# Weights of the projections split by two DMAs from DRAM, in place of a load, a copy and a subtraction

## The chip, the cores and the metric

The kernel runs on one core of one Trainium2 chip. The metric is the device time of one execution in microseconds: a median of 1206.1 us over three runs (1205.3 to 1206.65) before the change. Times, spans and rows come from one profiled execution, unless a text says that they are of the runs.

## The reference: what is computed

One encoder block over 1024 tokens of width 1024, in float32. The tokens form a grid of 16 rows by 64 columns.

```
n    = rmsnorm(h) ; proj = n @ w_in                    # 1024 x (3072 + 32) columns
y_na = neighbourhood attention of proj's qa, ka, va    # 8 heads x 64
y_gl = bidirectional gated linear attention            # 4 heads, chunks of 64 tokens
h    = h + concat(y_na, y_gl) @ w_out
h    = h + square(relu(rmsnorm(h) @ w_ff1)) @ w_ff2    # 4096 wide
out  = rmsnorm(h)
```

## The kernel before

**Products in parts.** TensorE works on operands of the type F32R, which holds fewer bits than float32. Each operand is therefore kept as a high part (the value rounded to F32R) and a low part (what the rounding left over, again as F32R), and each product is three matmuls: high by high, high weight by low data, low weight by high data (`product`). In names, `wh` and `wl` are the parts of a weight block, `nh` and `nl` those of the normed input, `y` those of the mixer's output.

**Blocks of weights.** The columns of `w_in` and of `w_out` lie in DRAM as blocks of 128 columns, each 128 partitions by 1024 float32 (512 KB): 24 blocks of `w_in` and 8 of `w_out`. A block of `w_in` serves two halves of 512 tokens with 24 matmuls each (`proj`; tile name `proj`). The output projection (`sums`; tile name `op`) goes through the 8 blocks of `w_out` twice, once for each half of the tokens: in the first pass with 21 matmuls a block, since the last of the eight slices of its input is left out until it is ready, in the second with 24. The missing slice is added between the passes from a rearranged tile of its own (tile name `opl`, weights loaded at L905 and split by `split`).

**How a block is made.** `weights` loads it into a float tile `wf` (a DMA from SP, L165) and calls `split`: ScalarE copies it to `wh` (L173), which rounds, and GpSimd, or VectorE in three cases, writes `wl = wf - wh` (L174). `wf`, `wh` and `wl` have two buffers each, in the pool `stg`. So `wf` of a block can be loaded while two earlier blocks are still in use, and its parts can be written when TensorE is through with the block before the last one. Two blocks of `w_in` at the start, and the rearranged slice, go through `load_w` or L905 and `split` without `weights`.

**Order of the work.** TensorE's instructions stand in the order in which the program is written. On the other engines a scheduler sets the order by priorities; what is written under `tc.high_priority(offset=SOON_W)` goes in as if it had been written some 100 instructions earlier. Each engine then works through its own instructions in order, and so do the DMA queues: SP's, which carries nearly all loads, and GpSimd's, whose DMAs stand in one line with its arithmetic.

**Stages.** Up to 44 us the input is split and normed and the first two blocks are projected. Then the linear attention runs head by head, with projections of later blocks put between its steps (`Fill`) so that TensorE has work while VectorE and ScalarE are at gates, scans and norms (to about 262 us). The neighbourhood attention follows in the same manner, in four pairs of heads (to about 441 us), and beside its last pair the first pass of the output projection begins. From about 465 us on the output projection stands nearly alone, until 545 us; the MLP takes the rest, from weight tiles (`A`) of its own that SP loads. GpSimd sums the squares for the second norm in the middle of the output projection (L880), as soon as VectorE has added a slice to `hT` and ScalarE has squared it.

Of the kernel before, what the change touches and what calls it, by code (L numbers as in the profile page):

```python
# [10 lines left out]
F32 = mybir.dt.float32  # L11
F32R = mybir.dt.float32r
U32 = mybir.dt.uint32
AF = mybir.ActivationFunctionType
ALU = mybir.AluOpType
# [3 lines left out]
P = 128  # L19
D = 1024  # L20
# [43 lines left out]
def block_kernel(ctx, tc, xT, g_mix, w_in, w_z, rpb, na_mask, gu, gb, g_gla, sel_f, sel_b,  # L64
                 rst, w_out, g_ff, w1, w2, g_fin, out):
    nc = tc.nc
    V, S, DMA, G = nc.vector, nc.scalar, nc.sync, nc.gpsimd
# [11 lines left out]
    stg = stg_stack.enter_context(pool("stg", L, 2))  # L79
# [81 lines left out]
    def weights(block, eng=None):  # L161

        with tc.high_priority(offset=SOON_W):
            wf = stg.tile([P, D], F32, tag="wf", name="wf")
            DMA.dma_start(wf, block)  # L165
            return split(wf, eng)

    def split(wf, eng=None, steps=1):
        wh = stg.tile([P, D], F32R, tag="wh", name="wh")
        wl = stg.tile([P, D], F32R, tag="wl", name="wl")  # L170
        for i in range(steps):
            c = slice(i * D // steps, (i + 1) * D // steps)
            S.copy(wh[:, c], wf[:, c])  # L173
            (eng or V).tensor_tensor(wl[:, c], wf[:, c], wh[:, c].bitcast(F32), op=ALU.subtract)  # L174
        return wh, wl
# [51 lines left out]
    def proj(blk, evac):  # L227

        w = weights(w_in[blk], G)
        for hf in range(2):  # L230
            d = bank("mm", f"proj{blk}_{hf}")
            yield from proj_part(d, w, hf * H, H)
            evac(hf, d)
# [437 lines left out]
    def sums(hf, d, ks, eng=None, w=None, ahead=()):  # L671

        w = w or weights(w_out[d], eng)
        o = bank("mm", f"op{hf}_{d}")
        for i, _ in enumerate(out_mm(o, hf, w, ks)):
            to_parts(hf, ahead[i:i + 1], G)
            yield
        add(hf, d, o)
# [220 lines left out]
    yhl[1] = half(a3, "y1")  # L899
    fill.run()  # L900
    w10 = weights(w_out[0], G)

    wf = stg.tile([P, D], F32, tag="wf", name="wf")
# [581 lines left out]
```

## Time and profile before

| what | profiled execution |
|---|---|
| time of this execution | 1203.34 us (the runs' median is 1206.1) |
| span of the core | 1201.6 us |
| TensorE busy | 1156.0 us, 96% |
| VectorE, ScalarE, GpSimd busy | 896.8, 646.3, 282.6 us |
| GpSimd's subtractions at L174 | 36, 88.8 us, 2467 ns each on the mean |
| loads of `wf` by SP | 38 of 512 KB through `weights`; 4 of 256 KB and 1 of 512 KB by others |
| moved by all DMAs | 73.02 MB, mean 61 GB/s |
| of that, by GpSimd's queue | 0.93 MB |
| granted TensorE clock, mean | 0.991 |

The rows are read so: a group's row names line, engine and operation, what is written and read, the count, then busy time, the mean of one in ns, and the idle time of that engine just before. A row of the order of time has start and duration in us, and in square brackets the idle time ahead of it and what ended it. A matmul's duration of some 0.39 us is longer than the distance between two starts, since matmuls are pipelined. In a row of a stretch stand its bounds, its length, then each engine's busy time with its count of instructions (TensorE's matmuls, its weight loads, VectorE, ScalarE, GpSimd), the granted TensorE clock, the DMA engines' share and GB/s.

### The profile page before, as it was taken

The page shows a single profiled execution, that of the slowest core. Times are in us where ns is not written, and L with a number is a line of the kernel's source. Part 1 is how long each engine was busy: PE and PEld are TensorE (multiplying, and loading weights), DVE is VectorE, ACT ScalarE, POOL GpSimd, SP SyncE. Part 2 cuts the span into 40 slices and gives each one's busy share as a digit, 9 for nine tenths or more (in the row PEclk, how much of TensorE's full clock was granted, in tenths as well). Part 3 has the DMA queues.
Part 4 walks back from the last instruction along what each step waited for, and adds up shares of the span by engine and source line. Part 5 has one row for each costly group of instructions (what it writes and reads, how often), then busy time and mean ns, then how long its engine had stood idle before and what let it go on. Part 6 is the DMA issues. An engine that isn't in the chain of part 4 may idle for free.

```text
span 1201.6 us, 15423 instructions
## 1 busy us (share of the span) xinstructions
PE 1156.0 (96%) x5632; PEld 946.8 (79%) x5632; DVE 896.8 (75%) x1558; ACT 646.3 (54%) x1201; POOL 282.6 (24%) x199
## 2 busy tenths in 40 slices
PE   9998999899999999999999999999999999999995
PEld 8877777687877878877778888888888888888775
DVE  8787778767868785695858885877859768597467
ACT  6766565545555665444643635546355463454654
POOL 5311101122131323530103230412304114041003
PEclk9999999999999999999999999999999999999998
DMA  7111010110111142230210122111211122111203
GB/s 236 50 58 52 25 36 19 35 57 19 49 36 49 32 156 92 104 123 1 70 59 26 58 70 69 35 55 53 71 53 35 53 70 70 53 36 53 71 1 140
DMA packets 37259, 73.02 MB, mean 61 GB/s; under 512 B 8928, under 2 KB 20320, under 8 KB 37184
## 3 DMA queue, kind: packets, MB, share of 16 engines
q1 hardware_dynamic: 36608, 71.11, 17.7%
q8 instruction: 44, 0.72, 0.2%
q0 software_dynamic: 432, 0.93, 0.2%
q14 instruction: 31, 0.25, 0.1%
q10 hardware_dynamic: 144, 0.00, 0.0%
HBM read 67.84 MB, written 5.96 MB: 61 GB/s over the span
## 4 chain that ended last, share of the span: by engine, by line
PE 70%; DVE 18%; ACT 8%; issue 2%; DMA 1%; SPq 0%; POOL 0%; DVEq 0%; ACTq 0%
PE f L111 24%; PE u L111 21%; PE proj L111 12%; PE op L111 5%; PE sc L111 2%; PE no L111 2%; PE pt L116 1%; DVE st L569 1%; DVE nl L284 1%; DVE b L492 1%; DVE b L490 1%; DVE st L566 1%; DVE pl L958 1%; DVE nf L888 1%; DVE fsq L1388 1%
## 5 line engine op out<-in xcount | busy, mean ns | idle before, releaser
L958 POOL TENSOR_TENSOR ul<-uB,uh 128x512 fp32r<-128x512 f32 x84 | 109.2, 1319 | 330.4 <-ACT uh L993 213.4
L980 ACT CAST ph<-A 128x512 fp32r<-128x512 f32 x166 | 103.0, 621 | 146.2 <-PE f L111 73.6
L174 POOL TENSOR_TENSOR wl<-wf,wh 128x1024 fp32r<-128x1024 f32 x36 | 88.8, 2467 | 333.8 <-ACT wh L173 310.6
L111 PE MATMUL f<-uh,ph 128*128 128x512 f32 x400 | 155.8, 390 | 1.5 <-ACT u L1001 1.4
L111 PE MATMUL f<-ul,ph 128*128 128x512 f32 x400 | 155.7, 389 | 0.1
L111 PE MATMUL f<-uh,pl 128*128 128x512 f32 x400 | 155.7, 389 | 0.0
L958 DVE TENSOR_TENSOR pl<-A,ph 128x512 fp32r<-128x512 f32 x166 | 112.8, 689 | 52.6 <-ACT ph L980 52.6
L111 PE MATMUL proj<-nh,wh 128*128 128x512 f32 x352 | 150.9, 429 | 0.8 <-DVE qd L255 0.8
L111 PE MATMUL proj<-nh,wl 128*128 128x512 f32 x352 | 139.6, 397 | 0.0
L111 PE MATMUL proj<-nl,wh 128*128 128x512 f32 x352 | 139.4, 396 | 0.0
L1140 DVE TENSOR_TENSOR hT<-hT,f 128x512 f32<-128x512 f32 x168 | 113.0, 687 | 19.9 <-PE f L111 19.9
L111 PE MATMUL u<-n,ph 128*128 128x512 f32 x288 | 89.2, 391 | 2.0 <-ACT ph L893 2.0
L111 PEld LDWEIGHTS f<-uh,ph 128*128 128x128 f32 x400 | 75.1, 188 | 17.9 <-ACT u L1001 1.8
L111 PEld LDWEIGHTS f<-ul,ph 128*128 128x128 f32 x400 | 75.1, 188 | 16.0 <-DVE ul L958 0.4
L111 PEld LDWEIGHTS f<-uh,pl 128*128 128x128 f32 x400 | 75.1, 188 | 15.6
L111 PEld LDWEIGHTS proj<-nh,wh 128*128 128x128 f32 x352 | 66.9, 190 | 19.8 <-issue 5.2
L993 ACT CAST uh<-uB 128x512 fp32r<-128x512 f32 x84 | 51.9, 618 | 51.3 <-PE f L111 34.5
L111 PE MATMUL u<-T,ph 128*128 128x512 f32 x256 | 79.2, 391 | 0.1
L111 PEld LDWEIGHTS proj<-nh,wl 128*128 128x128 f32 x352 | 67.1, 191 | 15.2
L111 PEld LDWEIGHTS proj<-nl,wh 128*128 128x128 f32 x352 | 67.4, 191 | 11.5 <-issue 1.4
L111 PE MATMUL op<-y,wh 128*128 128x512 f32 x240 | 75.8, 396 | 0.4 <-DVE y L665 0.4
L111 PE MATMUL u<-nt,ph 128*128 128x512 f32 x224 | 68.9, 389 | 0.0
(297 smaller groups left out, 2484.5 us busy)
## 6 DMA issues: line engine op xcount, KB each, us to landing
A<-in_w SPq DMA_DIRECT2D x64, 512.0 KB
wf<-in_w_in SPq DMA_DIRECT2D x22, 512.0 KB
wf<-in_w_out SPq DMA_DIRECT2D x17, 512.0 KB
hT<-in_xT SPq DMA_DIRECT2D x2, 2048.0 KB
xs<-in_xT SPq DMA_DIRECT2D x6, 512.0 KB
out<-hT SPq DMA_DIRECT2D x4, 512.0 KB
out<-hT SPq DMA_DIRECT2D x8, 256.0 KB
rpb<-rpb SPq DMA_DIRECT2D x16, 96.0 KB
```

What stands on the lines that cost most here:

```text
L111: m = nc.tensor.matmul(*args, **kw)
L116: tc.keep_in_program_order(nc.tensor.transpose(*args, **kw))
L174: (eng or V).tensor_tensor(wl[:, c], wf[:, c], wh[:, c].bitcast(F32), op=ALU.subtract)
L284: V.scalar_tensor_tensor(nl[:, k, sl], xs[:, k, :], gmix[:, k:k + 1], nh[:, k, sl].bitcast(F32), op0=ALU.mult, op1=ALU.subtract)
L490: V.tensor_tensor_scan(b[0:64, c], rsts[0:64, :], m[0:64, :], 0.0, op0=ALU.mult, op1=ALU.add)
L492: V.tensor_tensor_scan(b[64:128, c][:, ::-1], rsts[64:128, ::-1], m[64:128, ::-1], 0.0, op0=ALU.mult, op1=ALU.add)
L566: V.scalar_tensor_tensor(st[0:64, i + 1, :], st[0:64, i, :], dec[0:64, i:i + 1], st[0:64, i + 1, :], op0=ALU.mult, op1=ALU.add)
L569: V.scalar_tensor_tensor(st[64:128, j - 1, :], st[64:128, j, :], dec[64:128, j:j + 1], st[64:128, j - 1, :], op0=ALU.mult, op1=ALU.add)
L958: return kp(eng.tensor_tensor(l, x, h.bitcast(F32), op=ALU.subtract))
L980: kp(S.copy(ph, x))
L993: kp(S.copy(uh, x))
L1140: kp(V.tensor_tensor(hT[:, d, c], hT[:, d, c], o[:, s], op=ALU.add))
```

## The change

`weights` no longer loads a float tile and no longer calls `split`. A DMA from GpSimd's queue brings the block from DRAM into `wh` and casts it to F32R on the way. ScalarE writes `-wh` into `wl`. A second DMA from GpSimd's queue reads the same block from DRAM once more and adds it to what stands in `wl`, so that `wl` becomes block minus high part. The argument that named the engine of the subtraction is not used any more. `split` stays as it is for the two blocks at the start and for the rearranged slice. All 38 calls of `weights` are changed: 22 for `w_in`, 16 for `w_out`.

```
     def weights(block, eng=None):
 
         with tc.high_priority(offset=SOON_W):
-            wf = stg.tile([P, D], F32, tag="wf", name="wf")
-            DMA.dma_start(wf, block)
-            return split(wf, eng)
+            wh = stg.tile([P, D], F32R, tag="wh", name="wh")
+            wl = stg.tile([P, D], F32R, tag="wl", name="wl")
+            G.dma_start(wh, block)
+            S.activation(wl, wh.bitcast(F32), AF.Copy, scale=-1.0)
+            G.dma_start(wl, block, accum_op=ALU.add)
+            return wh, wl
```

The line numbers behind `weights` move up by 3 (L174 becomes L177, L880 becomes L883).

GpSimd in the output projection, before: the last low parts ahead of the sums of squares, and the first of the seven sums (`acc` is the sum, `sq` a square).

```order
L174 TENSOR_TENSOR wl<-wf,wh 128x1024 [waits DMAHW3_49,PE_49,Activation_49]
L174 TENSOR_TENSOR wl<-wf,wh 128x1024 [waits DMAHW4_49,PE_49,Activation_49]
L174 TENSOR_TENSOR wl<-wf,wh 128x1024 [waits DMAHW5_49,PE_49,Activation_49]
L880 TENSOR_TENSOR acc_4603<-acc_4603,sq_4610 128x512 [waits Activation_49]
L880 TENSOR_TENSOR acc_4603<-acc_4603,sq_4618 128x512 [waits Activation_49,Pool_49]
L880 TENSOR_TENSOR acc_4603<-acc_4603,sq_4626 128x512 [waits Activation_49,Pool_49]
```

The same place now, from the slice's subtraction (L177) to the end of the sums.

```order
L177 TENSOR_TENSOR wl<-wf,wh 128x1024 [waits DMASW4_49,DMAHW0_49,PE_49,Activation_49]
L166 DMA wh<-in_w_out 128x1024 [waits DMASW5_49,PE_49]
L883 TENSOR_TENSOR acc_4572<-acc_4572,sq_4579 128x512 [waits Activation_49]
L883 TENSOR_TENSOR acc_4572<-acc_4572,sq_4587 128x512 [waits Activation_49,Pool_49]
L168 DMA wl<-in_w_out 128x1024 [waits DMASW6_49,Activation_49]
L166 DMA wh<-in_w_out 128x1024 [waits DMASW3_49,PE_49]
L883 TENSOR_TENSOR acc_4572<-acc_4572,sq_4595 128x512 [waits Activation_49,Pool_49]
L883 TENSOR_TENSOR acc_4572<-acc_4572,sq_4603 128x512 [waits Activation_49,Pool_49]
L883 TENSOR_TENSOR acc_4572<-acc_4572,sq_4611 128x512 [waits Activation_49,Pool_49]
L883 TENSOR_TENSOR acc_4572<-acc_4572,sq_4619 128x512 [waits Activation_49,Pool_49]
L883 TENSOR_TENSOR acc_4572<-acc_4572,sq_4627 128x512 [waits Activation_49,Pool_49]
L168 DMA wl<-in_w_out 128x1024 [waits Activation_49]
```

Where one subtraction stood for a block, two DMAs stand, high part and low part in turn, and the sums of squares now lie between the two DMAs of a block: two of the seven in the first pair, five in the second.

ScalarE at the end of the last attention pair, before: the copies to `wh` between the attention's casts (`pt`) and copies (`otmp`).

```order
L173 CAST wh<-wf 128x1024 [waits DMAHW0_49,PE_49,Pool_49]
L782 CAST pt_3936<-pt_7_0_4375 128x2x128 [waits PE_49,Activation_49]
L782 CAST pt_3938<-pt_7_1_4380 128x2x128 [waits PE_49,Activation_49]
L173 CAST wh<-wf 128x1024 [waits DMAHW1_49,PE_49,Pool_49]
L173 CAST wh<-wf 128x1024 [waits DMAHW2_49,PE_49,Pool_49]
L812 COPY otmp<-no_0_1_4344 64x512 [waits PE_49]
L812 COPY otmp<-no_1_1_4347 64x512 [waits PE_49]
```

And now: the negations, which wait for GpSimd's DMAs (`DMASW`).

```order
L167 ACTIVATE wl<-wh 128x1024 [waits DMASW5_49,DMASW2_49,PE_49]
L785 CAST pt_3914<-pt_7_0_4349 128x2x128 [waits PE_49,Activation_49]
L785 CAST pt_3916<-pt_7_1_4354 128x2x128 [waits PE_49,Activation_49]
L167 ACTIVATE wl<-wh 128x1024 [waits DMASW7_49,DMASW4_49,PE_49]
L815 COPY otmp<-no_0_1_4319 64x512 [waits PE_49,Activation_49]
L167 ACTIVATE wl<-wh 128x1024 [waits DMASW6_49,DMASW1_49]
L815 COPY otmp<-no_1_1_4322 64x512 [waits PE_49,Activation_49]
```

Here one negation stands an instruction later than its copy did. The matmuls are the same, in the same order.

## The prediction

> **What bounds the kernel now.** I read the page's busy times and its chain first, then the busy times by stretch of the program, then the waits of the weights' tiles.
>
> ```profile
> PE 1156.0 (96%) x5632; PEld 946.8 (79%) x5632; DVE 896.8 (75%) x1558; ACT 646.3 (54%) x1201; POOL 282.6 (24%) x199
> PE 70%; DVE 18%; ACT 8%; issue 2%; DMA 1%; SPq 0%; POOL 0%; DVEq 0%; ACTq 0%
> core 0: us, PE busy (x) PEld busy (x) DVE busy (x) ACT busy (x) POOL busy (x), PEclk, DMA share, GB/s
> 44.00:262.00 218.00, 200.73 (x1113) 160.64 (x1112) 167.76 (x262) 127.79 (x206) 39.62 (x28) 0.97 0.12 39
> 262.00:441.00 179.00, 176.34 (x909) 141.03 (x909) 141.06 (x386) 106.62 (x266) 42.45 (x24) 1.00 0.14 44
> 441.00:465.00 24.00, 23.60 (x125) 18.69 (x125) 18.99 (x55) 14.46 (x40) 7.79 (x4) 1.00 0.60 218
> 465.00:545.00 80.00, 77.03 (x340) 62.38 (x338) 52.66 (x63) 35.49 (x53) 36.92 (x19) 1.00 0.28 99
> ```
>
> TensorE sets the end: busy 96%, and 70% of the chain. The four stretches are the linear attention with its projections (44 to 262 us), the neighbourhood attention with its own (to 441), and the output projection, first beside the last attention work (to 465) and then alone (to 545). TensorE idles 17 us in the first (218 less 200.7) and 3 us in each of the second and the last. So little can be gained, and whatever makes TensorE wait for a weight shows in full.
>
> When is a weight late? Its two parts live in two buffers each, so the block after next can be made only when a block's last matmul is through. The time left is one block's length on TensorE.
>
> ```profile
> 263.60 1.05 ACT L173 CAST wh<-wf 128x1024 fp32r<-128x1024 f32 x1 [1.95 <-PE proj L111]
> 276.67 1.05 ACT L173 CAST wh<-wf 128x1024 fp32r<-128x1024 f32 x1 [0.69 <-PE proj L111]
> 312.33 1.05 ACT L173 CAST wh<-wf 128x1024 fp32r<-128x1024 f32 x1
> 328.60 1.05 ACT L173 CAST wh<-wf 128x1024 fp32r<-128x1024 f32 x1 [1.97 <-PE proj L111]
> 448.14 1.05 ACT L173 CAST wh<-wf 128x1024 fp32r<-128x1024 f32 x1 [1.17 <-PE op L111]
> 455.76 1.05 ACT L173 CAST wh<-wf 128x1024 fp32r<-128x1024 f32 x1 [1.92 <-issue]
> 491.15 1.05 ACT L173 CAST wh<-wf 128x1024 fp32r<-128x1024 f32 x1 [3.71 <-PE op L111]
> 496.60 1.05 ACT L173 CAST wh<-wf 128x1024 fp32r<-128x1024 f32 x1 [4.39 <-PE op L111]
> 492.29 2.39 POOL L174 TENSOR_TENSOR wl<-wf,wh 128x1024 fp32r<-128x1024 f32 x1 [2.37 <-ACT wh L173]
> 477.97 0.39 PE L111 MATMUL op<-y,wl 128*128 128x512 f32 x1
> 478.20 0.40 PE L111 MATMUL op<-y,wh 128*128 128x512 f32 x1
> PE op L111 <- POOL wl L174: 2.8, 2, 1.8
> ```
>
> ScalarE's copies that waited for TensorE mark the releases. In the projections of the attention they are 13 to 16 us apart (263.60 to 276.67, 312.33 to 328.60), because attention work runs between a block's matmuls; where the output projection begins, 7.6 (448.14 to 455.76); and later there 5.45 us (491.15 to 496.60), which is 24 matmuls of 0.23 us (478.20 less 477.97). Today's chain fits even there: the float weight lies ready, the copy takes 1.05 and GpSimd's subtraction, 0.09 behind it, 2.39, in all 3.5 us. TensorE waits 2.8 us for it in the last stretch.
>
> **The change part by part.** It removes 38 loads on SP, 35 subtractions on GpSimd and 3 on VectorE. ScalarE's 38 copies become 38 negations of the same size. GpSimd's queue gets 76 DMAs of 512 KB, strictly high part, low part, high part; nothing can be fetched ahead of the release any more. The new chain from release to use is a DMA, a negation and a second DMA.
>
> The trace has no casting and no adding DMA. The nearest rows are the plain ones on GpSimd's queue:
>
> ```profile
> guf<-in_gu POOLq DMA_DIRECT2D x1, 256.0 KB, 6.3
> rsts<-in_rst POOLq DMA_DIRECT2D x1, 256.0 KB, 8.5
> msk<-in_na_mask POOLq DMA_DIRECT2D x1, 256.0 KB, 3.4
> selF<-in_sel_f POOLq DMA_DIRECT2D x1, 64.0 KB, 3.4
> selB<-in_sel_b POOLq DMA_DIRECT2D x1, 64.0 KB, 3.1
> 0.00:25.00 25.00, 22.53 (x133) 20.76 (x133) 20.07 (x35) 18.35 (x39) 15.50 (x17) 1.00 0.88 281
> ```
>
> The mask's 256 KB took 3.4 us in a quiet stretch; guf and rsts took 6.3 and 8.5 in the first 25 us, where the DMA engines were 88% busy at 281 GB/s. At that rate 256 KB more are 0.93 us.
> - Casting DMA: 3.4 + 0.93 = 4.3 us. Low end 3.1 (selB), high end 9.4 (rsts and 0.93). I take 4.3, since the mask was moved beside the same work.
> - Negation: 1.05 us, some 0.1 of handover on each side, 0.25 for ScalarE's queue: 1.5.
> - Adding DMA: it must read the old value too. Second stream free: 4.3; both streams in turn: 3.4 - 0.93 + 4 x 0.93 = 6.2; high end 9.4 again. I take 5.8, nearer the doubled stream.
>
> Together 11.6 us; TensorE can run two matmuls with the high part first, so 11.1 count.
>
> *The Trainium skill, "DMA: Bandwidth & Descriptors", section "Anatomy of one DMA — SWDGE (gpsimd) path", fits such a DMA as 2.0 us plus the bytes at 436 GB/s. By that fit each DMA would be an estimated 3.2 us, which is a rival below; for the mask it gives 2.6, and the row above says 3.4.*
>
> Attention projections, 44 to 441 us: 13 to 16 us are there and 11.1 are needed, so 0; the cover is the attention work between a block's matmuls. Without it the length would be 48 matmuls of 0.23, 11.0 us, and the chain would just show. Behind an adding DMA that waits, GpSimd's queue holds the clearing of state tiles and the low parts of the next queries; GpSimd is busy 40 of 218 us and 42 of 179 there, so I cost that at nothing.
>
> The first block behind the opening has no cover:
>
> ```profile
> L111 PE MATMUL sb<-nh,wl x32: 279/283/415, 11.4 to 36.8; 128*128 128x256 f32 x32
> L111 PE MATMUL proj<-nh,wl x352: 387/393/632, 44.2 to 436.5; 128*128 128x512 f32 x176
> ```
>
> Its buffer comes free at 37.1, and its low part was first used at 44.2. New: 37.1 + 11.6 = 48.7, so 4.5 us late. **+4.5.**
>
> The output projection alone, 465 to 545:
>
> ```profile
> 465.00:545.00 80.00, 66.64 (x214) 39.93 (x214) 5.55 (x3) 13.39 (x13) 24.04 (x10) 1.00 0.28 99
> ```
>
> This is the same stretch for the instructions on the high part alone: 214 matmuls, which are 5 blocks of 14, 8 of 16 and the last slice of 16, so 14 blocks in 80 us, 5.7 each. With two buffers, each cycles through chain and use, and the two take turns: a block per (11.1 + 5.7)/2 = 8.4 us, 2.7 more. The slice is still made from a float tile by the old chain, which spares about one of the 13: 12 x 2.7 = 32. Ahead of it, from 441 to 465, one of the three blocks has only those 7.6 us and waits 3. **+35.** The 2.8 us waited there now are part of it: **-2.8.**
>
> GpSimd's order adds a wait of its own: the second block of the second half has its adding DMA behind five of the seven sums of squares.
>
> ```profile
> 500.62 10.41 POOL L880 TENSOR_TENSOR acc<-acc,sq 128x512 f32<-128x512 f32 x7 [5.95 <-ACT sq L878]
> ```
>
> They ended at 511 and start no earlier now, while that block's negation would let the DMA go at some 508.5 (release at 502, 4.3, 1.5, queue). Between 0 and 5; I take 2.5, and behind it in the queue stands the next block's casting DMA. **+2.5.**
>
> The clock: TensorE's waits have a price beyond themselves. The first two rows are stretches of 3.4 us.
>
> ```profile
> 235.50:238.90 3.40, 1.36 (x6) 0.77 (x5) 3.14 (x9) 0.00 (x0) 0.54 (x1) 1.00 0.00 0
> 238.90:242.30 3.40, 2.30 (x15) 2.01 (x16) 3.18 (x7) 0.00 (x0) 0.00 (x0) 0.50 0.00 0
> 243.81 0.63 PE L111 MATMUL proj<-nh,wl 128*128 128x512 f32 x1
> 244.24 0.63 PE L111 MATMUL proj<-nh,wh 128*128 128x512 f32 x1
> ```
>
> After 3.4 us with TensorE busy 1.36, the granted clock was 0.50 and matmuls started 0.43 apart. 3.4 us at that clock lose 1.6 us of work. New waits are 5.4 us for each pair of blocks (11.1 less 5.7), some 6 pairs: between 0 and 6 x 1.6 = 10; I take half. **+5.** *"TensorE: Matmul & The Clock Gate", section "HAM oscillation — how this bites in real kernels", of the Trainium skill has the same rule (no idle gaps above some 3.4 us); by it the whole 10 would be the estimate.*
>
> VectorE is relieved:
>
> ```profile
> 144.38 1.22 DVE L490 TENSOR_TENSOR_SCAN b<-rsts,lm 64x512 f32<-64x512 f32 x1
> 147.59 3.43 DVE L490 TENSOR_TENSOR_SCAN b<-rsts,lm 64x512 f32<-64x512 f32 x1
> 56.90 3.26 DVE L492 TENSOR_TENSOR_SCAN b<-rsts,lm 64x512 f32<-64x512 f32 x1
> 147.56 2.38 POOL L174 TENSOR_TENSOR wl<-wf,wh 128x1024 fp32r<-128x1024 f32 x1 [20.05 <-DVE lm L489]
> ```
>
> Beside GpSimd's subtraction a scan takes 3.4 instead of 1.2. Two such lie in the chain of waits, 4.2 us; between 0 and 9 (half of TensorE's 17 us of idling there). I take **-3.** The SP loads that go cost nothing now, being ahead of need.
>
> Sum: 4.5 + 35 - 2.8 + 2.5 + 5 - 3 = 41. The profiled execution took 1203.3 (span 1201.6), so 1244.5; the median of the runs, 1206.1, stands 2.8 above it: **1247 us**.
>
> **Rivals.**
> 1. *The adding DMA is slow.* At 9.4 the chain is 14.7: (14.7 + 5.7)/2 = 10.2, 4.5 x 12 = 54, 6.5 for the block before, 8 at the start, some 4 in the projections that have only 13 us, then the same 2.5 + 5 - 5.8: +74, **1280**; with a casting DMA of 6 about **1300**. For it: no row shows an add, and guf and rsts were slow. Against: those two ran beside the opening's loads.
> 2. *ScalarE is held.* It works in order, and the negation now waits 4.3 us longer for data than the copy did for a release. Where it stands too early, attention's exponentials and evictions queue behind it: some 1 us for each of the 22 blocks, +22, **1270**. For it: copies that waited for TensorE at 328.60. Against: the new order puts the negations a few instructions later than the copies.
> 3. *Short DMAs.* Both land in some 3.2 us, close to selB's row: the cast costs nothing and the second stream of the add is free. The chain counts 7.4 (two DMAs and 1.5, less 0.5), a block takes 6.55: 0.85 x 12 = 10, start 1, order and clock 2, less 5.8: +7, **1213**. Against: eight times selB's bytes, and the mask's 3.4 for half of them. *This is where the fit of the Trainium skill named above would put it.*
> 4. *VectorE's relief wins.* With both at selB's 3.1 the chain counts 7.2 and the output projection loses 9; the whole 9 of the relief's upper end and the 2.8 stand against it: -3, **1203**. It decides only if both DMAs land within 3.1 us and the scans' 2 us lie wholly on TensorE's path.
>
> **How the numbers follow.** Forecast (chain shows in the output projection alone) 0.62, slow add 0.18, ScalarE 0.10, short DMAs 0.06, relief 0.04. The forecast's own range: both DMAs at 4.3 and no clock loss give a chain of 9.7, 2 x 12 = 24, 3, 2, 2.5 - 5.8: 1232; an add at 7.5 and the full clock loss give 13, 3.6 x 12 = 43, 6.5, 5, 2.5 + 10 - 5.8: 1267. Reaching to the others, 1217 to 1298 leaves out the relief, most of the short DMAs and the far end of the slow add. Differences of 0.2%, 2.4 us, can just be told from none here. Only the relief makes it faster: 0.04; within 0.2%: 0.02; slower: 0.94.
>
> **What would show it.** From 465 us on, TensorE's idle time should be named as waiting for the weights' DMAs, in turns of long and short, with blocks some 8.4 us apart, and the stretch near 115 us long; from 44 to 441 nearly no such wait, but for one of 4 to 5 us at the start. The landing times of the two kinds of DMA on GpSimd's queue decide the sizes: 4.3 and 5.8. It is wrong if the adding DMAs land in over 8 us, if waits for weights fill the attention stretch too, or if ScalarE's waits for casting DMAs stand in the chain.

## The result, and the profile after

The changed kernel takes **1250.7 us** (median of 4 runs, 1248.9 to 1253.0) against 1205.7 us of the kernel before in its 4 runs: a ratio of **1.0379** (95% interval 1.0353 to 1.0406), slower by 45.0 us. 1247 had been forecast, 1217 to 1298 as the range. The profiled execution took 1250.25 us, its span is 1248.5 us, 46.9 longer than before.

Where the 46.9 us lie is read from the first matmul of the output projection (`op`) and the first of the MLP (`u`). Before:

```profile
L111 PE MATMUL op<-y,wh x240: 387/389/799, 441.8 to 544.2; 128*128 128x512 f32 x120
L111 PE MATMUL u<-n,ph x288: 387/389/799, 546.9 to 1108.2; 128*128 128x512 f32 x144
```

After:

```profile
L111 PE MATMUL op<-y,wh x240: 387/389/799, 438.1 to 588.8; 128*128 128x512 f32 x120
L111 PE MATMUL u<-n,ph x288: 387/389/799, 591.4 to 1154.4; 128*128 128x512 f32 x144
```

| part | before | after | difference |
|---|---|---|---|
| to the first `op` | 441.8 | 438.1 | -3.7 |
| first `op` to first `u` | 105.1 | 153.3 | **+48.2** |
| first `u` to the end | 654.7 | 657.1 | +2.4 |

So all of it, and a little more, was lost in the output projection, and the attention in front of it became shorter. The 2.4 us behind the first `u` need not come from the output projection: in two kernels below that leave it as it was (`w_in` alone, and that but for its first block), this last part takes 656.2 and 656.9 us. The loss in the output projection shows in the busy times by stretch of the program too (the last two stretches are the output projection alone):

```profile
44.00:262.00 218.00, 201.36 (x1117) 160.83 (x1118) 154.23 (x261) 127.76 (x206) 26.28 (x41) 0.97 0.30 65
262.00:441.00 179.00, 177.48 (x922) 142.91 (x921) 132.66 (x393) 109.95 (x274) 33.80 (x37) 1.00 0.34 82
441.00:465.00 24.00, 19.96 (x94) 15.05 (x93) 14.15 (x43) 11.18 (x32) 4.05 (x5) 0.93 0.75 208
465.00:545.00 80.00, 61.88 (x234) 47.92 (x232) 21.54 (x36) 23.38 (x37) 23.18 (x25) 0.87 0.53 129
545.00:592.00 47.00, 33.60 (x120) 25.44 (x120) 18.96 (x29) 14.97 (x23) 7.64 (x9) 0.89 0.43 97
```

From 465 to 545 us TensorE was busy 77.0 us with 340 matmuls; now it is busy 61.9 with 234, at a mean clock of 0.87 in place of 1.00. In the first two stretches VectorE needs 154.2 and 132.7 us where it had needed 167.8 and 141.1.

What TensorE waits for there, by the view of waits (us in total, times, longest):

```profile
PE op L111 <- DMA wl<-in_w_out: 33.2, 12, 5.3
PE proj L111 <- DMA wl<-in_w_in: 5.6, 1, 5.6
```

Before, 2.8 us stood in the place of the 33.2, and the second row did not exist. These are the two places that the prediction named. And the new DMAs, from issue to landing (median):

```profile
wh<-in_w_in POOLq DMA_DIRECT2D x22, 512.0 KB, 3.8
wl<-in_w_in POOLq DMA_DIRECT2D x22, 512.0 KB, 5.4
wh<-in_w_out POOLq DMA_DIRECT2D x16, 512.0 KB, 4.5
wl<-in_w_out POOLq DMA_DIRECT2D x16, 512.0 KB, 5.3
```

By these medians a casting DMA of 512 KB lands in 3.8 to 4.5 us, one that adds in 5.3 to 5.4. The next rows show the second pass of the output projection: first TensorE's first use of the low part in each of the last five blocks (the idle time before it in square brackets), then VectorE's addition behind each second block (L686).

```profile
547.65 0.50 PE L111 MATMUL op<-y,wl 128*128 128x512 f32 x1 [3.66 <-DMA wl<-in_w_out]
555.55 0.50 PE L111 MATMUL op<-y,wl 128*128 128x512 f32 x1 [0.56 <-DMA wl<-in_w_out]
565.13 0.64 PE L111 MATMUL op<-y,wl 128*128 128x512 f32 x1 [3.84 <-DMA wl<-in_w_out]
573.59 0.50 PE L111 MATMUL op<-y,wl 128*128 128x512 f32 x1 [1.12 <-DMA wl<-in_w_out]
582.57 0.80 PE L111 MATMUL op<-y,wl 128*128 128x512 f32 x1 [3.22 <-DMA wl<-in_w_out]
```

```profile
536.98 0.69 DVE L686 TENSOR_TENSOR hT<-hT,op 128x512 f32<-128x512 f32 x1 [12.92 <-PE op L111]
554.57 0.69 DVE L686 TENSOR_TENSOR hT<-hT,op 128x512 f32<-128x512 f32 x1 [4.94 <-PE op L111]
572.06 0.69 DVE L686 TENSOR_TENSOR hT<-hT,op 128x512 f32<-128x512 f32 x1 [6.09 <-PE op L111]
589.42 0.69 DVE L686 TENSOR_TENSOR hT<-hT,op 128x512 f32<-128x512 f32 x1 [8.15 <-PE op L111]
```

Long and short waits take turns, and a pair of blocks takes 17.4 to 17.6 us, 8.7 to 8.8 a block. That is the two-buffer cycle of the prediction, with 8.4 forecast.

Around each of the longer waits (2.35 us and more) the clock falls. Three of the eight stretches at half clock in the output projection:

```profile
459.50:462.90 3.40, 3.40 (x11) 2.44 (x10) 1.73 (x5) 2.36 (x5) 0.86 (x1) 0.50 0.23 17
503.90:510.70 6.80, 6.04 (x14) 4.78 (x15) 0.00 (x0) 1.06 (x1) 0.87 (x1) 0.50 0.34 66
548.30:551.70 3.40, 3.40 (x10) 2.64 (x9) 1.34 (x2) 2.08 (x3) 0.87 (x1) 0.50 0.01 4
```

Together the eight are 34.0 us with 83 matmuls; before, the output projection had none. TensorE counts as busy in them, so its slow matmuls appear in no list of waits.

### The profile page after: what moved, and what is told of

Read it like the earlier page. It is cut to its first block, busy times and chain, and to the rows that moved or that the text cites. A ratio compares the mean times of both kernels' runs of the same rounds, so it can differ in the third digit from the quotient of the medians.

```text
span 1248.5 us, 15424 instructions
## 1 busy us (share of the span) xinstructions
PE 1173.5 (94%) x5632; PEld 956.6 (77%) x5632; DVE 856.2 (69%) x1555; ACT 647.0 (52%) x1201; POOL 247.0 (20%) x240
## 4 chain that ended last, share of the span: by engine, by line
PE 67%; issue 10%; DVE 9%; ACT 6%; DMA 4%; POOL 2%; SPq 0%; DVEq 0%; POOLq 0%; ACTq 0%
PE f L111 23%; PE u L111 21%; PE proj L111 14%; PE sc L111 1%; PE op L111 1%; PE o L111 1%; DMA wl<-in_w_out 1%; PE pt L116 1%; PE no L111 1%; DVE st L572 1%; DMA wh<-in_w_out 1%; DMA wh<-in_w_in 1%; DVE asb L564 1%; DVE pl L961 1%; POOL wl L168 1%
## 5 line engine op out<-in xcount | busy, mean ns | idle before, releaser
L111 PEld LDWEIGHTS f<-uh,ph 128*128 128x128 f32 x400 | 75.1, 188 | 17.8 <-ACT u L1004 1.8
L111 PE MATMUL op<-y,wh 128*128 128x512 f32 x240 | 85.8, 441 | 0.3 <-DVE y L668 0.3
L111 PE MATMUL op<-y,wl 128*128 128x512 f32 x120 | 54.6, 455 | 33.2 <-DMA wl<-in_w_out 33.2
L111 PEld LDWEIGHTS proj<-nl,wh 128*128 128x128 f32 x352 | 67.1, 191 | 11.6 <-issue 1.4
```

The costliest lines, as they stand in the source:

```text
L111: m = nc.tensor.matmul(*args, **kw)
```

## The experiments

Ratios are against the kernel before on the same chip in the same session; its median was 1203.5 to 1205.8 us there.

### Each half of the change alone

`weights` was given an argument that chooses between the old making of a block and the new one; the first kernel sets it for `w_in`, the second for `w_out`.

```
-    def weights(block, eng=None):
+    def weights(block, eng=None, two=False):
...
+            if not two:
+                wf = stg.tile([P, D], F32, tag="wf", name="wf")
+                DMA.dma_start(wf, block)
+                return split(wf, eng)
...
-        w = weights(w_in[blk], G)
+        w = weights(w_in[blk], G, True)
```

> The 22 blocks of w_in are made by the two DMAs, the 16 of w_out by load, copy and subtraction as before. My theory: the loss lies in the output projection alone (there the changed kernel took from 438.1 to some 589.4 us, before it was 441.8 to 545), and the attention stretch became 3.7 us shorter although TensorE waited 5.6 us at its start for the first low part. So this kernel should be no slower than before: 1199 to 1204 us. Rival: the attention stretch gained only because the order of the work shifted, and the wait at the start stays: 1208 to 1212 us.

> The other half: only the 16 blocks of w_out are made by the two DMAs. My theory: the whole loss, 1250 to 1257 us, slower than the changed kernel by the 3 us that the attention stretch gains there. Rival (attention and output projection each lose half): some 1228 us.

`w_in` alone: **1203.3 us**, ratio 0.9993 (0.9982 to 1.0004). `w_out` alone: **1253.9 us**, 1.0413 (1.0397 to 1.0430). The theory holds in both, and the rivals fall: the loss is not spread over both kinds of blocks. In the kernel with `w_in` alone the output projection takes 105.1 us, as before. The two differences are -1.3 and +49.4 us, in sum 48.1 where the whole change showed 45.0; the 3 us lie about within the intervals.

### `w_in` alone, but for the first block behind the opening

Why does the change of `w_in` come out at nothing? By the theory the late first block takes back what VectorE gains.

```
-        w = weights(w_in[blk], G, True)
+        w = weights(w_in[blk], G, blk != 4)
```

> As with w_in alone, but its first block behind the opening (the values of head 0) is made by load, copy and subtraction. My theory: the wait of 5.6 us for the first low part goes, and with it the 6.8 us at a granted clock of 0.50 behind it (3 us lost): 1191 to 1198 us, faster than before, and 6 to 9 faster than w_in alone. Rival (the wait is hidden anyway, since VectorE sets the end of that stretch): the same as w_in alone within 2 us.

**1196.8 us**, 0.9939 (0.9925 to 0.9953): faster than both kernels. The late first block therefore costs 6.5 us, and the change of the other 21 blocks brings 7.8 (1204.55 less 1196.77). That VectorE's relief is what brings them is tested next. In the profile the first `op` starts at 433.6 us, where it was 441.8 before:

```profile
L111 PE MATMUL op<-y,wh x240: 387/389/799, 433.6 to 536.1; 128*128 128x512 f32 x120
```

### What the relief is: idle work on GpSimd

Three kernels put back work on GpSimd that nobody uses, in the kernel of 1196.8 us, 21 times: a subtraction as long as the one removed, which reads 128x1024; two clearings of a spare tile, which read nothing; and two clearings of the low part's own buffer ahead of its negation.

```
+            dm = stg.tile([P, D], F32, tag="wf", name="dm")                                  # first
+            G.tensor_tensor(dm, wh.bitcast(F32), wh.bitcast(F32), op=ALU.subtract)
...
+            dm = stg.tile([P, D], F32, tag="wf", name="dm")                                  # second
+            G.memset(dm, 0.0)
+            G.memset(dm, 0.0)
...
             G.dma_start(wh, block)                                                           # third
+            for _ in range(2):
+                G.memset(wl.bitcast(U32), 0)
```

> As with w_in but for its first block, and GpSimd does one subtraction of 128x1024 for each of the 21 blocks again, of the high part from itself into a tile that nobody reads; the adding DMA goes out up to 2 us later, which 13 to 16 us of room cover. My theory: what the attention stretch gained is that GpSimd no longer reads beside VectorE, so the gain goes: 1201 to 1206 us, 6 to 12 above the kernel without these subtractions, with VectorE's scans of 3.4 us back. Rival (the gain comes from SP's loads or ScalarE's order): within 2 us of the kernel without them.

> The kernel with w_in changed but for its first block behind the opening and w_out as before (1196.8 us), with idle work on GpSimd as in the run with idle subtractions (1206.3 us), but work that reads nothing: for each of the 21 blocks two clearings of a spare 128x1024 float tile, some 1.1 us each, that nobody reads. Theory (GpSimd's reading beside VectorE slows VectorE, and the subtractions' reading was worth the 9.5 us): 1196 to 1200 us, with VectorE busy some 157 us from 44 to 262 us as without idle work. Rival (GpSimd's time in its queue delays the next block's DMAs, whatever it does in it): 1202 to 1206 us.

> The kernel with w_in changed but for its first block behind the opening and w_out as before (1196.8 us), again with idle work on GpSimd that reads nothing, but now tied to its place: for each of the 21 blocks two clearings of the buffer of the low part, some 1 us each, between the casting DMA and the negation that overwrites it, so that they can't pile up at the start as the clearings of a spare tile did (all of them ran before 75 us). They lie beside the casting DMA's 3.8 us and so delay no adding DMA. Theory (what VectorE suffers from is GpSimd's reading, not its writing): 1195.5 to 1199.5 us, and VectorE's state updates at 360 to 370 ns on the mean as without idle work, not 381 and 423. Rival (any GpSimd work in these stretches costs what the subtractions cost, 0.45 us a block): 1203 to 1207 us.

The subtractions: **1206.3 us**, 1.0021 (1.0007 to 1.0034), 9.5 more than without them. The size is the theory's, a little past its end, but the sign that it named did not appear: the scans stayed at 1.2 us. What slowed instead were other VectorE instructions, in this stretch above all the state updates. Without idle work, from 44 to 262 us, and then with the idle subtractions:

```profile
L576 DVE SCALAR_TENSOR_TENSOR st<-st,dec 64x128 f32<-64x128 f32 x56 | 20.6, 367 | 1.9
L573 DVE SCALAR_TENSOR_TENSOR st<-st,dec 64x128 f32<-64x128 f32 x56 | 20.2, 361 | 6.3 <-ACT st L552 4.3
```

```profile
L578 DVE SCALAR_TENSOR_TENSOR st<-st,dec 64x128 f32<-64x128 f32 x56 | 23.7, 423 | 1.9
L575 DVE SCALAR_TENSOR_TENSOR st<-st,dec 64x128 f32<-64x128 f32 x56 | 21.3, 381 | 6.1 <-ACT st L554 4.2
44.00:262.00 218.00, 201.68 (x1101) 161.06 (x1100) 161.79 (x257) 125.14 (x203) 49.45 (x52) 0.95 0.30 63
```

With the clearings of the low part's buffer, where GpSimd is busy even longer (51.6 us):

```profile
L578 DVE SCALAR_TENSOR_TENSOR st<-st,dec 64x128 f32<-64x128 f32 x56 | 20.6, 369 | 1.9
L575 DVE SCALAR_TENSOR_TENSOR st<-st,dec 64x128 f32<-64x128 f32 x56 | 20.2, 361 | 6.2 <-ACT st L554 4.3
44.00:262.00 218.00, 204.31 (x1138) 163.19 (x1137) 155.89 (x264) 129.53 (x210) 51.57 (x68) 0.98 0.32 71
```

423 and 381 ns are, within 1 ns, what the kernel before shows for the same updates; 369 and 361 are, within 2 ns, those without idle work. Over the whole execution VectorE is busy 874.1 us without idle work, 889.7 with the subtractions, and 874.7 and 876.8 with the clearings of the third and the second kernel. So GpSimd's reading slows VectorE, and its writing hardly does: the third kernel takes **1198.9 us**, 0.9958 (0.9942 to 0.9974), where the theory said 1195.5 to 1199.5 and the rival 1203 to 1207. *The Trainium skill, "SBUF — State Buffer", section "Who interferes with whom", states this rule: an instruction of VectorE with two inputs in SBUF contends with an instruction of GpSimd that reads, not with one that only writes. The rows of the state updates, which have two inputs in SBUF, agree.* Clearings need not be free for all of VectorE: two kinds of instruction with one tensor input were longer in these two runs, the small copies to `bl` in the second kernel (432 ns on the mean instead of 171) and the scalings `xsc` in the third (2.9 us more in sum).

The second kernel, **1201.6 us**, 0.9974 (0.9960 to 0.9988), lies between both ranges and settles less: its clearings waited for nothing, so all 42 ran before 75 us. There a casting DMA left at 58.49 instead of 55.05 us and TensorE waited 2.8 us for VectorE at 75.8.

A delay of the weights in GpSimd's queue, the other thing that idle work could do, is not what costs the 9.5 us: with the idle subtractions TensorE waits once for a low part of `w_in` from 44 to 441 us, 2.1 us, and without them once, 2.5 us. But VectorE need not be the whole of it either: TensorE is at half clock for 20.4 us between 44 and 262 us with the idle subtractions, and for 6.8 without them. How much is the one and how much the other was not separated.

### The clock: TensorE kept busy through the long waits

Fourteen matmuls into a bank that nobody reads stand ahead of the first low part in every second block of the second pass, some 3.2 us where TensorE would have waited.

```
+            for _ in range(busy if k == ks[0] else 0):
+                PE.matmul(spare, a, h, start=True, stop=True)
             PE.matmul(dst, b, h, start=False, stop=last and k == ks[-1])
...
+        for i, _ in enumerate(out_mm(o, hf, w, ks, 14 if hf and d % 2 else 0)):
```

> The changed kernel, and in four blocks of the second pass of the output projection (the odd ones, whose waits for the low part were 5.3, 3.7, 3.8 and 3.2 us) 14 more matmuls, whose product nobody reads, between the second matmul and the first that needs the low part: 3.2 us of work at the full clock inside the wait. My theory: these waits cost more than themselves, since behind them the granted clock stood at 0.50 for 6.8, 3.4, 3.4 and 3.4 us; kept busy, the clock stays at 1.00 there, and the kernel becomes 4 to 9 us faster than the changed one in spite of 56 more matmuls: 1242 to 1247 us. Rival (the clock costs nothing, since the chain of DMAs sets the end): 1250 to 1253 us.

**1247.3 us**, 1.0359 (1.0328 to 1.0390): 3.4 less than the change, 0.3 short of the theory's range. The interval overlaps that of the changed kernel, so the runs alone don't tell the gain from none; the rows do show one. From 527 us on the half clock shrank from 17.0 us to 3.4, and two blocks take 16.0 to 17.0 us (L690 is the addition):

```profile
539.55 0.69 DVE L690 TENSOR_TENSOR hT<-hT,op 128x512 f32<-128x512 f32 x1 [12.03 <-PE op L111]
556.40 0.68 DVE L690 TENSOR_TENSOR hT<-hT,op 128x512 f32<-128x512 f32 x1
572.44 0.69 DVE L690 TENSOR_TENSOR hT<-hT,op 128x512 f32<-128x512 f32 x1 [6.12 <-PE op L111]
589.40 0.69 DVE L690 TENSOR_TENSOR hT<-hT,op 128x512 f32<-128x512 f32 x1 [6.47 <-PE op L111]
```

So with the clock kept up a block costs 8.0 to 8.5 us, where the prediction had 8.4, and the half clock adds some 0.4 to it. The six blocks of these rows take 49.85 us instead of 52.44. That is little for 13.6 us less at half clock: a block that runs faster waits longer for the next weight. In the second pass TensorE still waits 8.9 us beside the extra matmuls, which take some 12.9 (56 at 0.23); without them it waited 17.7.

### A third pair of buffers

Blocks 1, 4 and 7 of the second pass get buffers of their own, so the chain has two blocks' time there.

```
+            if pool:
+                wh = pool.tile([P, D], F32R, tag="wh3", name="wh3", bufs=1)
+                wl = pool.tile([P, D], F32R, tag="wl3", name="wl3", bufs=1)
...
+        w = w or weights(w_out[d], eng, yp if hf and d % 3 == 1 else None)
```

> The changed kernel with a third pair of buffers for the weights in the second pass of the output projection (blocks 1, 4 and 7 of that pass use it). My theory: the loss is the chain from release to use against the length of one block; with three buffers the room is two blocks, some 11 us, against a chain of 11 to 12, and nearly all waits of that pass go: 1226 to 1234 us. Rival: GpSimd's queue sets the pace, because an adding DMA waits for the negation and holds what stands behind it (6.2 us for a block at the least, and the sums of squares): waits remain, 1240 to 1250 us.

**1239.0 us**, 1.0287 (1.0255 to 1.0319), 11.8 less, between the ranges of the theory and the rival. TensorE's waits in the second pass fell from 17.7 to 8.3 us. What is left goes with GpSimd's order, in which low and high parts still take turns here:

```profile
541.91 0.87 POOL L172 DMA_DIRECT2D wl<-in_w_out  x1 [4.24 <-ACT wl L171]
542.45 0.89 POOL L170 DMA_DIRECT2D wh<-in_w_out  x1
550.18 0.87 POOL L172 DMA_DIRECT2D wl<-in_w_out  x1 [6.84 <-ACT wl L171]
552.91 0.54 POOL L170 DMA_DIRECT2D wh<-in_w_out  x1 [1.86 <-PE op L111]
```

An adding DMA holds the queue until its negation is done, which waits for the casting DMA just ahead; the casting DMA of the next block stands behind, even where its buffer is free (the one at 542.45 left without a wait of its own, the one at 552.91 waited 1.86 us for TensorE). At the last block of the first pass, which has no third pair, a casting DMA took 8.7 us and TensorE waited 7.9, where it was 4.8 in the changed kernel. Another casting DMA, which had waited for no matmul and so went into a fresh buffer, the third pair's, had left 1.3 us ahead of it (489.92 and 491.21 us), and its adding DMA 2.3 us ahead (499.09 and 501.37). So the third pair seems to have moved a part of the wait into the first pass.

### The casting DMA without the adding one

Here the blocks of `w_out` have a float tile, which SP loads ahead, a casting DMA for the high part, and a subtraction: in the first kernel on GpSimd, in the second on VectorE (with the blocks of `w_in` as in the kernel of 1196.8 us).

```
+            if cast:
+                wf = stg.tile([P, D], F32, tag="wf", name="wf")
+                DMA.dma_start(wf, block)
+                wh = stg.tile([P, D], F32R, tag="wh", name="wh")
+                wl = stg.tile([P, D], F32R, tag="wl", name="wl")
+                G.dma_start(wh, block)
+                (eng or V).tensor_tensor(wl, wf, wh.bitcast(F32), op=ALU.subtract)   # second kernel: V
+                return wh, wl
```

> The blocks of w_in as in the change; for the blocks of w_out only the casting DMA is kept: SP loads a float tile ahead of need, the casting DMA makes the high part, and GpSimd subtracts (low = float tile less high part), so negation and adding DMA are gone. Theory (what costs is the length of the chain from release to use against a block's 5.7 us): casting DMA 4.5 us, handover 0.1, subtraction 2.4, less the 0.5 that TensorE can run ahead, 6.5; a block every (6.5 + 5.7)/2 = 6.1 us, 0.4 more in 12 places, 5 us, and a few of clock on top of the 1203 us that the blocks of w_in alone gave: 1206 to 1214 us, and TensorE's waits in the output projection under 10 us. Rival (each of the two DMAs brings its share of the loss, by its own time in the queue): about half of the 48 us of the output projection stays, 1224 to 1231 us.

> The blocks of w_in as in that kernel of 1196.8 us; the blocks of w_out with the casting DMA for the high part, a float tile loaded ahead by SP, and the subtraction on VectorE. With the subtraction on GpSimd the same blocks had come every 7.4 us (casting DMA 4.9, subtraction 2.4, one behind the other in GpSimd's order, so that the next casting DMA left only behind the subtraction). Theory (that order was the limit, and the chain itself is short enough: 4.8 and 0.1 and some 1.2 on VectorE, less 0.5, 5.6 against a block's 5.7): the loss in the output projection goes, 1196 to 1203 us. Rival (casting DMAs in the output projection cost by themselves, beside SP's loads, whoever subtracts): 1212 to 1220 us.

GpSimd subtracting, but for the three blocks that VectorE does as before: **1225.7 us**, 1.0162 (1.0133 to 1.0190). The theory's 1206 to 1214 falls, and the number lies where the rival had put it. The rival's reason (a share for each of the two DMAs) is not what the trace shows: there the DMA and the subtraction stand one behind the other on GpSimd.

```profile
474.29 0.56 POOL L169 DMA_DIRECT2D wh<-in_w_out  x1
479.52 2.34 POOL L170 TENSOR_TENSOR wl<-wf,wh 128x1024 fp32r<-128x1024 f32 x1 [4.68 <-PE op L111]
481.81 0.57 POOL L169 DMA_DIRECT2D wh<-in_w_out  x1
486.72 2.90 POOL L170 TENSOR_TENSOR wl<-wf,wh 128x1024 fp32r<-128x1024 f32 x1 [4.33 <-issue]
489.56 0.56 POOL L169 DMA_DIRECT2D wh<-in_w_out  x1
```

474.29, 481.81, 489.56: a block every 7.5 to 7.8 us, though the buffers would allow 6.1 by the expectation's estimate. The subtraction waits at the head of the queue for its own DMA, and the next block's DMA stands behind it. With the subtraction on VectorE: **1205.9 us**, 1.0021 (1.0001 to 1.0040). The output projection then takes 114.8 us (432.9 to 547.7) instead of 125.3 (442.6 to 567.9), so of the 20.2 us above 105.1 about half goes, and 9.7 stay. The theory's range ended 3 us short of the number, so its rival (casting DMAs cost by themselves) is not wholly wrong: some loss stays, whoever subtracts. Of the 9.7 us, 5.9 are idle time of TensorE (11.16 us instead of 5.23 in the output projection) and 3.8 are longer busy time. The waits are of some 1 us each, since the chain (4.3 us for the DMA by its median, 1.2 on VectorE) leaves little room in a block of 5.7:

```profile
481.95 0.50 PE L111 MATMUL op<-y,wl 128*128 128x512 f32 x1 [0.90 <-DVE wl L172]
499.05 0.50 PE L111 MATMUL op<-y,wl 128*128 128x512 f32 x1 [1.17 <-DVE wl L172]
505.44 0.73 PE L111 MATMUL op<-y,wh 128*128 128x512 f32 x2 [1.11 <-DMA wh<-in_w_out]
```

The shorter subtraction and the freed order came together in this kernel, so their shares are not told apart.

### A faster version

The kernel of 1196.8 us still waited once for a low part, that of the second block behind the opening.

```
-        w = weights(w_in[blk], G, blk != 4)
+        w = weights(w_in[blk], G, blk not in (4, 8))
```

> The kernel with w_in changed but for its first block behind the opening, and w_out as before (1196.8 us); now the second block behind the opening is made in the old way too. In that kernel TensorE waited 2.46 us for that block's low part at 58.3 us, its adding DMA having stood behind two others on GpSimd's queue, and ran at half clock for 3.4 us behind it. Theory (that wait and its clock are on TensorE's path): 2.5 and some 1.6 less, 0.5 more for the subtraction's reading: 1192 to 1195 us. Rival (the linear attention's gates and scans end no earlier, so the time is taken back there): 1196 to 1198.5 us.

**1195.2 us**, 0.9906 (0.9889 to 0.9923), the fastest here. The number lies between the two ranges, 0.2 us above the theory's. The wait of 2.46 us went, but one of 1.65 us for VectorE came 12 us later, and the first `op` starts at 432.5 us, 1.1 earlier, as the rival has it. The size of the gain stays open: 1.5 us by the two medians, which are of different sessions, and 4 us by the two ratios (0.9906 and 0.9939).

## Why the prediction was right, and which terms were not

**The bound and the mechanism were right.** The time lies 3.7 us above the forecast of 1247 and inside its own range of 1232 to 1267. The change costs where a block on TensorE is shorter than the chain from release to use, the output projection, and the first block behind the opening; in the other attention projections no wait for weights appeared.

**The chain.** Casting 4.3 forecast, 3.8 to 4.5 measured; adding 5.8 forecast, 5.3 to 5.4 measured; so with the negation's 1.5 some 10.7 us for the blocks of `w_in` and 11.3 for those of `w_out`, against 11.6. Reading the mask's DMA and scaling it by the bytes was good for the cast, and the doubled stream a little too dear for the add. One reading was loose: of the four distances that the prediction took for releases, the 16 and the 7.6 us lean on copies at 312.33 and 455.76 us whose rows name no wait for TensorE, so those two are no measured releases. *The fit of the Trainium skill's page "DMA: Bandwidth & Descriptors", section "Anatomy of one DMA — SWDGE (gpsimd) path", an estimated 3.2 us, is below both kinds here (3.8 and 5.4).* Rival 1 (a slow add, 9.4) and rival 3 (3.2 for both) fall with these rows.

**The output projection: mis-sized.** The terms were 35 - 2.8 for the waits, 2.5 for GpSimd's order and 5 for the clock, 39.7 in sum; the profile shows 48.2. TensorE's waits for low parts grew by 30.4 us (33.2 less 2.8), near the 32.2. The remaining 17.8 are longer busy time of TensorE (117.7 us instead of 99.9 for the same 461 matmuls), and slower matmuls are the larger part of that. At 0.23 us apart the 83 matmuls of the half-clock stretches need 19.1 us; TensorE was busy with them for 31.8 of the 34.0, so some 12.7 us lie there. The other 5 were not taken apart. The prediction took 5 of at most 10, half of six stretches of 3.4 us at 1.6 each; there were ten such lengths in eight stretches, two of them double where waits of 4.82 and 5.25 us stood (504.66 and 529.04 us). In the steady turns themselves the sum holds: 8.7 us a block instead of 8.4, and 8.0 to 8.5 when the clock was kept up. How much of the 17.8 a clock kept up would give back over both passes was not measured; over the six blocks of the rows above it was 2.6.

One casting DMA also took 6.4 us beside SP's loads for the MLP, which the term didn't have. ScalarE's order of time:

```profile
505.95 1.06 ACT L167 ACTIVATE wl<-wh 128x1024 fp32r<-128x1024 f32 x1 [8.41 <-DMA wh<-in_w_out]
521.90 1.06 ACT L167 ACTIVATE wl<-wh 128x1024 fp32r<-128x1024 f32 x1 [0.37 <-DMA wh<-in_w_out]
530.32 1.06 ACT L167 ACTIVATE wl<-wh 128x1024 fp32r<-128x1024 f32 x1 [0.53 <-DMA wh<-in_w_out]
```

**GpSimd's order: 2.5 forecast, 0.4 measured.** The five sums of squares ended just as the negation did:

```profile
524.87 6.99 POOL L883 TENSOR_TENSOR acc<-acc,sq 128x512 f32<-128x512 f32 x5
531.79 0.88 POOL L168 DMA_DIRECT2D wl<-in_w_out  x1
```

The negation ended at 531.38, the DMA left at 531.79. The output projection ran late by then, so the squares were ready in time. The two sums in the pair ahead held its adding DMA a little longer, 0.75 us (its negation ended at 522.96, the DMA left at 523.71). What the prediction did not see is that the queue's order can delay every block, not this one alone: the adding DMA holds it while its negation waits. With two buffers this is hidden behind the release; the third pair of buffers brought it out.

**The first block: 4.5 forecast, 6.5 measured.** Its low part was used at 49.5 us instead of 44.2, 5.3 late, and 6.8 us at half clock followed (from 46.5 us). The wait was near, 0.8 us too short; its clock was not in the term.

**VectorE's relief: 3 forecast, 7.8 measured.** The step read only the two slow scans. Many instructions of VectorE beside a reading GpSimd were slower, which the sum of VectorE's busy time from 44 to 441 us shows (22 us less) and the means of the state updates, but the scans' rows alone don't. The upper end of 9 held.

**The sum.** 4.5 - 3 + 39.7 stood for 41; 6.5 - 7.8 + 49.4, from the experiments, stands for 48, and 45.0 was measured. That the forecast came as near as it did is in part luck: a relief that was too small by 4.8 stood against an output projection too small by 8.5 to 9.7 and a start too small by 2. Rival 2 (ScalarE held) does not show in the time: ScalarE waits 11.2 us for casting DMAs of `w_in` from 44 to 438 us, 2.8 at most at a time, and the attention became shorter. Rival 4's mechanism, the relief, is real and nearly its full size, but could not win against the chain; where the change is left out in the output projection and at the first blocks, the relief makes the kernel faster than before.

## What to carry to other kernels

Count the chain from a buffer's release to its next use, in DMAs and handovers, against the time of one block in the shortest stage that uses it: the same change was worth -8 us where a block had 13 us or more (without the first block, which had no such room) and +49 where it had 5.7. Where a queue that is worked through in order holds a step that waits for the result of the step just ahead of it, what stands behind can't be fetched early, even with a buffer free for it. An engine's relief is read from the busy time of all its instructions in a stretch, not from the few that stand out.

## What was not expected of the hardware

- An adding DMA of 512 KB (5.3 to 5.4 us) is only 0.8 to 1.6 us longer than a casting one (3.8 to 4.5) by the medians, though it needs the old value too.
- A subtraction of GpSimd, 2.4 us long, can cost the kernel 0.45 us (9.5 us for 21) by way of VectorE and TensorE's clock, while two clearings that together take as long cost 0.1 (2.1 us for 21 pairs, within the spread of the runs).
- The half clock also came where TensorE had not been idle for the whole 3.4 us before it. It was busy for 1.46 and 0.65 us there, at waits of 2.49 and 3.66 us. *The rule that the prediction names from the Trainium skill, "TensorE: Matmul & The Clock Gate", section "HAM oscillation — how this bites in real kernels" (no idle gaps above some 3.4 us), is too loose for the first of these.*

```profile
456.10:459.50 3.40, 1.46 (x8) 1.31 (x9) 2.00 (x8) 1.77 (x7) 0.00 (x0) 1.00 0.79 228
544.90:548.30 3.40, 0.65 (x3) 0.57 (x4) 1.46 (x3) 1.77 (x3) 0.00 (x0) 0.99 0.98 261
```
